# A batched fp32 matmul fed by one DMA queue: loads and stores queued in turns of four batches instead of one by one

## The chip, the cores and the metric

The kernel runs on one core of a Trainium2 chip, alone. The metric is device time in microseconds for one launch: 261.9 us before the change (median of three runs, 261.72 to 262.05). One execution was also recorded by the hardware profiler; it took 262.47 us, of which the profile shows a span of 260.7 us from the first to the last instruction.

## The reference

Sixteen independent products, each of a transposed 768 x 512 matrix with a 768 x 1024 matrix, in fp32:

```python
batch, m, k, n = 16, 512, 768, 1024
x: (batch, k, m)   y: (batch, k, n)
return np.einsum('bkm,bkn->bmn', x, y).astype(np.float32)
```

Per batch x is 1536 KB, y is 3072 KB and the output is 2048 KB. Over the whole run 75.5 MB are read and 33.55 MB are written.

## The kernel before, in words

The kernel goes through the 16 batches in order. No scheduler is at work: each engine has its own list of instructions, written out by hand, and the engines meet at semaphores.

- **SP** issues all the DMAs, on one queue (L102 to L113). For each batch b it issues the load of x into one of two fp32 buffers `xs` (L106), the load of y into one of two buffers `ys` (L109) and, from batch 4 on (`LAG`), the store of batch b-4 (L111, the function `store` at L93). Stores 11 to 14 follow the last load (11 in the loop, the others in L112), and the store of batch 15 is issued after the section (L181). [...]
- **VectorE** casts x and then y of each batch to bf16 (L124, L128) into one of two slots of `xb` and `yb`, and counts each cast in the semaphore `cast`. The load of x for batch b waits for the cast of x of batch b-2 (L105), and the same holds for y (L108), since they share a buffer. The cast of x for batch b waits until the matmuls of batch b-2 are done (L122), since they read the slot.
- **GpSimd** only turns the count `cast` into the semaphore `ready` for TensorE (L131 to L134).
- **TensorE** does 48 matmuls per batch, of 128 x 128 weights with 512 columns (L150), in two groups of 24, each filling one half of PSUM (`ps`). It waits for `ready` (L141, L148) and, per group, for `room` (L145), which says that this half has been copied out. Each finished group adds one to `groups`.
- **ScalarE** copies each half from PSUM into one of five output buffers `ob` (L166). For batch b from 5 on it first waits for the semaphore `so` of the store of batch b-5 (L163), which used the same buffer.
- `store(b)` waits until the matmuls of batch b+1 are done (L97), which implies that batch b was copied out; for batch 14 it waits for `outs` (L99). Before the last store SP waits for the stores 11, 12 and 13 (L174, L175).

`wide_dma` (L69) issues a load with long rows: a packet of x or y is 48 KB (four rows of x, two of y), one of a store 16 KB.

Of the kernel before, what the change touches and what calls it, by code (L numbers as in the profile page):

```python
# [1 line left out]

_os.environ.setdefault("NEURON_RT_ULTRASERVER_MODE", "4")

# [2 lines left out]

# [5 lines left out]


@with_exitstack
def kernel(
    ctx: ExitStack,
    tc: tile.TileContext,
    x: bass.AP,
    y: bass.AP,  # L20
    out: bass.AP,
):
    nc = tc.nc
    P = 128
    FP32 = mybir.dt.float32
    BF16 = mybir.dt.bfloat16

    B, K, M = x.shape
    _, _, N = y.shape
    KT = K // P  # L30
    MT = M // P
    NF = 512
    NT = N // NF

    x_v = x.rearrange("b (p ko) m -> b p ko m", ko=KT)
    y_v = y.rearrange("b (p ko) n -> b p ko n", ko=KT)
    o_v = out.rearrange("b (p mo) n -> b p mo n", mo=MT)

    LAG = 4
    NO = 5
    KH = KT // 2

    section = ExitStack()
    section.enter_context(tc.tile_critical())
    ec = ctx.enter_context
    xs = [ec(nc.sbuf_tensor(f"xs{i}", [P, KT, M], FP32)) for i in range(2)]
    ys = [ec(nc.sbuf_tensor(f"ys{i}", [P, KT, N], FP32)) for i in range(2)]
    xb = ec(nc.sbuf_tensor("xb", [P, 2, KT, M], BF16))  # L50
    yb = ec(nc.sbuf_tensor("yb", [P, 2, KT, N], BF16))
    ob = [ec(nc.sbuf_tensor(f"ob{i}", [P, MT, N], FP32)) for i in range(NO)]

    HB = MT // 2
    ps = [ec(nc.psum_tensor(f"ps{i}", [P, HB, NT, NF], FP32)) for i in range(2)]
    sx = [ec(nc.semaphore(f"sx{i}")) for i in range(2)]
    sy = [ec(nc.semaphore(f"sy{i}")) for i in range(2)]
    so = [ec(nc.semaphore(f"so{i}")) for i in range(NO)]
    cast = ec(nc.semaphore("cast"))
    ready = ec(nc.semaphore("ready"))  # L60
    room = ec(nc.semaphore("room"))
    groups = ec(nc.semaphore("groups"))
    idle = ec(nc.semaphore("idle"))
    outs = ec(nc.semaphore("outs"))


    made = {}

    def wide_dma(key, dst, src, dram_rows, load):  # L69


        if key not in made:
            made[key] = nc.sync.dma_start(dst, src)
            return made[key]
        pat = mybir.BassSymbolicTensorAccessPattern
        widen = lambda a: a.rearrange("(q r) k m -> q (r k m)", r=dram_rows)
        plain = lambda a: a.rearrange("p k m -> p (k m)")
        s, d = (widen(src), plain(dst)) if load else (plain(src), widen(dst))
        return nc.sync.add_instruction(_copy.replace(
            made[key].ins, name=nc.get_next_instruction_name(),  # L80
            ins=(pat(ap=s.ap, dtype=s.dtype, bass_ap=s, is_dma=False),),
            outs=(pat(ap=d.ap, dtype=d.dtype, bass_ap=d, is_dma=False),),
            sync_info=None, ant_dge_precooked=False))


    def parts(b):
        return 2 if b in (15,) else 1


    nx = [sum(1 + parts(a) for a in range(b)) + 1 for b in range(B)]  # L90


    def store(b):  # L93


        if b < B - 2:
            nc.sync.wait_ge(groups, 2 * (b + 2))  # L97
        else:
            nc.sync.wait_ge(outs, b - (B - 3))  # L99
        nc.sync.dma_start(o_v[b], ob[b % NO][:]).then_inc(so[b % NO], 16)  # L100

    for b in range(B):  # L102
        i = b % 2
        if b >= 2:
            nc.sync.wait_ge(cast, nx[b - 2])  # L105
        wide_dma("x", xs[i][:], x_v[b], 4, True).then_inc(sx[i], 16)  # L106
        if b >= 2:
            nc.sync.wait_ge(cast, nx[b - 2] + parts(b - 2))  # L108
        wide_dma("y", ys[i][:], y_v[b], 2, True).then_inc(sy[i], 16)  # L109
        if b >= LAG:  # L110
            store(b - LAG)  # L111
    for b in range(B - LAG, B - 1):  # L112
        store(b)  # L113


    for _ in range(60):
        nc.vector.sem_inc(idle, 1)
    for b in range(B):
        i = b % 2
        n = 16 * (b // 2 + 1)  # L120
        if b >= 2:
            nc.vector.wait_ge(groups, 2 * (b - 1))  # L122
        nc.vector.wait_ge(sx[i], n)
        nc.vector.tensor_copy(xb[:, i], xs[i][:]).then_inc(cast, 1)  # L124
        nc.vector.wait_ge(sy[i], n)
        for h in range(parts(b)):
            ks = slice(h * KT // parts(b), (h + 1) * KT // parts(b))
            nc.vector.tensor_copy(yb[:, i, ks], ys[i][:, ks]).then_inc(cast, 1)  # L128


    for b in range(B):  # L131
        nc.gpsimd.wait_ge(cast, nx[b]).then_inc(ready, 1)
        for h in range(parts(b)):
            nc.gpsimd.wait_ge(cast, nx[b] + h + 1).then_inc(ready, 2 // parts(b))  # L134


    x_w = xb[:].rearrange("p s k (j mo) -> p s k mo j", mo=MT)
    pe = OrderedEngineSet([nc.tensor.engine])
    with nc.Fori(0, B // 2, engines=pe):
        with nc.Fori(0, 2, engines=pe) as s:  # L140
            nc.tensor.wait_ge(ready, 2).then_inc(ready, -2)  # L141
            for mo in range(MT):
                g, m = divmod(mo, HB)
                if m == 0:
                    nc.tensor.wait_ge(room, 1).then_inc(room, -1)  # L145
                for kt in range(KT):
                    if mo == 0 and kt == KH:
                        nc.tensor.wait_ge(ready, 1).then_inc(ready, -1)  # L148
                    for nt in range(NT):
                        mm = nc.tensor.matmul(  # L150
                            ps[g][:, m, nt], x_w[:, bass.ds(s, 1), kt, mo],
                            yb[:, bass.ds(s, 1), kt, nt * NF:(nt + 1) * NF],
                            start=(kt == 0), stop=(kt == KT - 1))
                if m == HB - 1:
                    mm.then_inc(groups, 1)


    nc.scalar.nop().then_inc(room, 2)
    for _ in range(60):
        nc.scalar.sem_inc(idle, 1)  # L160
    for b in range(B):
        if b >= NO:
            nc.scalar.wait_ge(so[b % NO], 16 * (b // NO))  # L163
        for g in range(2):
            nc.scalar.wait_ge(groups, 2 * b + g + 1)
            cp = nc.scalar.copy(ob[b % NO][:, g * HB:(g + 1) * HB].rearrange("p m (t f) -> p m t f", f=NF),  # L166
                                ps[g][:])
            if b < B - 1:
                cp.then_inc(room, 1)
        if b == B - 2:  # L170
            nc.scalar.drain().then_inc(outs, 1)
    cp.then_inc(outs, 1)

    for b in range(B - LAG - 1, B - 2):  # L174
        nc.sync.wait_ge(so[b % NO], 16 * (b // NO + 1))  # L175
    section.close()

    nc.sync.dma_start(o_v[B - 1], ob[(B - 1) % NO][:])  # L181


# [1 line left out]
_INS = ['x', 'y']  # L185
_OUTS = [((16, 512, 1024), 'float32')]


# [23 lines left out]
```

## Time and profile before

| | |
|---|---|
| median of three runs | 261.9 us |
| the profiled execution | 262.47 us |
| its span | 260.7 us |
| DMA queue of SP | 109.05 MB, 98.1% of 16 engines' span |
| mean rate | 418 GB/s |
| TensorE matmul busy | 186.1 us (71%) |
| VectorE busy | 82.0 us (31%) |
| ScalarE busy | 61.1 us (23%) |
| mean granted TensorE clock | 0.911 |
| y load, x load, store: median issue to landing | 28.2, 29.7, 32.6 us |

The page divides the span into 40 slices and gives a digit of busy share for each engine and for the DMA engines. The timeline lists instructions by start time; the bracket behind a row gives how long the engine had been idle and what ended that. A cast that was released by "DMA ys<-in_y_dram" starts just as the y load has landed, so the start times of the casts are a clock for the queue.

### The profile page before, as it was taken

How to read it: one execution, taken by the hardware profiler on the slowest of the kernel's cores; microseconds unless marked ns; L12 is line 12 of the kernel's file. 1: busy time of each engine (PE TensorE's matmuls, PEld its weight loads, DVE VectorE, ACT ScalarE, POOL GpSimd, SP SyncE). 2: the span in 40 equal slices, each digit the busy share in tenths (PEclk: the TensorE clock that was granted, in tenths of full speed). 3: DMA queues.
4: the chain of work that ended last, by engine and by line, in shares of the span. 5: the costliest groups of instructions: out<-in, count | busy, mean ns of one | idle time of the engine just before them, and what ended most of it. 6: DMA issues, size and time to landing. Idle time of an engine off the chain costs nothing. (4 is left out here: it accounts for less than half of the span.)

```text
span 260.7 us, 2506 instructions
## 1 busy us (share of the span) xinstructions
PE 186.1 (71%) x768; PEld 89.8 (34%) x768; DVE 82.0 (31%) x33; ACT 61.1 (23%) x33; POOL 0.2 (0%) x4
## 2 busy tenths in 40 slices
PE   0009999998937949479596894969959197696910
PEld 0004555554512515124242351434425043253500
DVE  0261644525222252312524115252142522225000
ACT  1000442243220222202214022040322205022220
POOL 0000000000000000000000000000000000000000
PEclk9999999999995999959889797797999889799985
DMA  7998999999899899989999989999998999999994
GB/s 260 432 494 385 468 385 468 392 392 488 385 410 493 370 450 475 427 385 405 483 400 437 465 367 453 410 483 402 410 485 382 445 468 417 410 410 430 427 410 181
DMA packets 4514, 109.07 MB, mean 418 GB/s; under 512 B 768, under 2 KB 768, under 8 KB 768
## 3 DMA queue, kind: packets, MB, share of 16 engines
q1 hardware_dynamic: 4512, 109.05, 98.1%
q14 instruction: 2, 0.02, 0.0%
HBM read 75.50 MB, written 33.55 MB: 418 GB/s over the span
## 5 line engine op out<-in xcount | busy, mean ns | idle before, releaser
L150 PE MATMUL ps<-yb,xb 128*128 x768 | 186.1, 407 | 62.7 <-PEq L145 60.7
L150 PEld LDWEIGHTS ps<-yb,xb 128*128 x768 | 89.8, 117 | 158.5 <-issue 92.2
L166 ACT COPY ob<-ps 128x2048 f32<-128x2048 f32 x32 | 59.8, 1870 | 184.2 <-PE ps L150 184.2
L128 DVE CAST yb<-ys 128x6144 bf16<-128x6144 f32 (+1 forms) x17 | 53.8, 3171 | 87.7 <-DMA ys<-in_y_dram 87.7
L124 DVE CAST xb<-xs 128x3072 bf16<-128x3072 f32 x16 | 28.2, 1760 | 69.4 <-DMA xs<-in_x_dram 65.3
L166 ACT ACT_TABLE_LOAD x1 | 1.3, 1283 | 5.3 <-issue 5.3
L196 POOL MEMSET const-bfloat16-1.0<- 128x1 bf16 x1 | 0.1, 102 | 0.0
L196 POOL MEMSET const-uint8-127<- 128x1 uint8 x1 | 0.1, 102 | 0.0
L196 POOL MEMSET const-float32-1.0<- 128x1 f32 x1 | 0.1, 99 | 0.0
L196 POOL MEMSET const-float32-0.0<- 128x1 f32 x1 | 0.1, 98 | 0.2 <-issue 0.2
## 6 DMA issues: line engine op xcount, KB each, us to landing
ys<-in_y_dram SPq DMA_DIRECT2D x16, 3072.0 KB, 28.2
out_dram<-ob SPq DMA_DIRECT2D x16, 2048.0 KB, 32.6
xs<-in_x_dram SPq DMA_DIRECT2D x16, 1536.0 KB, 29.7
```

The lines of the kernel that those rows point to most:

```text
L124: nc.vector.tensor_copy(xb[:, i], xs[i][:]).then_inc(cast, 1)
L128: nc.vector.tensor_copy(yb[:, i, ks], ys[i][:, ks]).then_inc(cast, 1)
L150: mm = nc.tensor.matmul(ps[g][:, m, nt], x_w[:, bass.ds(s, 1), kt, mo], yb[:, bass.ds(s, 1), kt, nt * NF:(nt + 1) * NF], start=(kt == 0), ...
L166: cp = nc.scalar.copy(ob[b % NO][:, g * HB:(g + 1) * HB].rearrange("p m (t f) -> p m t f", f=NF), ps[g][:])
L196: nc = _bacc.Bacc("TRN2", target_bir_lowering=False, num_devices=1)
```

## The change

SP's order of DMAs is rewritten. The loads of batches 0 to 7 come first. Then four stores (0 to 3), the loads of 8 to 11, the stores of 4 to 7, the loads of 12 to 15, and the stores of 8 to 15 follow in turn, the last of them after the section as before. Each load and each store keeps the waits that it had; five output buffers and two load buffers remain. The waits ahead of the last store name the same three stores. No other engine's instructions change.

```diff
-    LAG = 4
+    FIRST = 8
+    TURN = 4
     NO = 5
...
-    for b in range(B):
+    def load(b):
         i = b % 2
         if b >= 2:
             nc.sync.wait_ge(cast, nx[b - 2])
...
         wide_dma("y", ys[i][:], y_v[b], 2, True).then_inc(sy[i], 16)
-        if b >= LAG:
-            store(b - LAG)
-    for b in range(B - LAG, B - 1):
+
+    for b in range(B):
+        load(b)
+        if b + 1 >= FIRST and (b + 1 - FIRST) % TURN == 0:
+            a = b + 1 - FIRST
+            for c in range(a, a + TURN):
+                store(c)
+    for b in range(B - FIRST + TURN, B - 1):
         store(b)
...
-    for b in range(B - LAG - 1, B - 2):
+    for b in range(B - NO, B - 2):
         nc.sync.wait_ge(so[b % NO], 16 * (b // NO + 1))
```

## The prediction

> **What bounds the kernel now.** I read the page first, its DMA rows above all, then the casts in the timeline as a clock for the queue, then the queue in stretches of 2 us, and last the tail of the timeline.
>
> ```profile
> span 260.7 us, 2506 instructions
> PE 186.1 (71%) x768; PEld 89.8 (34%) x768; DVE 82.0 (31%) x33; ACT 61.1 (23%) x33; POOL 0.2 (0%) x4
> ...
> DMA  7998999999899899989999989999998999999994
> ...
> q1 hardware_dynamic: 4512, 109.05, 98.1%
> ```
>
> The one queue fills 98.1% of 16 DMA engines' span; no compute engine passes 71%. The queue is the bound from the first load to the last store. So the order of its transfers can move the time in three ways only: the queue runs dry, the same bytes take longer or shorter, or the last store is issued late.
>
> The casts of y start when the load of y has landed (rows of batches 3 to 8, then of 12 and 13):
>
> ```profile
> 48.18 3.36 DVE L128 CAST yb<-ys 128x6144 bf16<-128x6144 f32 x1 [4.49 <-DMA ys<-in_y_dram]
> ...
> 59.71 3.36 DVE L128 CAST yb<-ys 128x6144 bf16<-128x6144 f32 x1 [5.67 <-DMA ys<-in_y_dram]
> ...
> 76.28 3.36 DVE L128 CAST yb<-ys 128x6144 bf16<-128x6144 f32 x1 [6.18 <-DMA ys<-in_y_dram]
> ...
> 92.76 3.36 DVE L128 CAST yb<-ys 128x6144 bf16<-128x6144 f32 x1 [6.10 <-DMA ys<-in_y_dram]
> ...
> 108.57 3.36 DVE L128 CAST yb<-ys 128x6144 bf16<-128x6144 f32 x1 [5.44 <-DMA ys<-in_y_dram]
> ...
> 124.86 3.36 DVE L128 CAST yb<-ys 128x6144 bf16<-128x6144 f32 x1 [5.93 <-DMA ys<-in_y_dram]
> ...
> 188.27 3.36 DVE L128 CAST yb<-ys 128x6144 bf16<-128x6144 f32 x1 [5.45 <-DMA ys<-in_y_dram]
> ...
> 204.06 3.36 DVE L128 CAST yb<-ys 128x6144 bf16<-128x6144 f32 x1 [5.45 <-DMA ys<-in_y_dram]
> ```
>
> While only loads run (y of batches 1, 2 and 3 at 26.19, 37.18, 48.18) a batch takes 11.00 us for 4.72 MB, 429 GB/s. With a store in it, the best periods are 15.81 (92.76 to 108.57) and 15.79 (188.27 to 204.06), so a store takes 4.8 us for 2.10 MB, about the same rate; the packet records of the five stores at the end give 4.85. An undisturbed mixed period is thus the plain sum: passing between loads and stores costs nothing as such. But some periods are longer: 11.53 instead of 11.00 to batch 4, then 16.57, 16.48, 15.81, 16.29, 15.83, 15.95 and no excess after that. Against 15.81 the excess is 0.53 + 0.76 + 0.67 + 0 + 0.48 + 0.02 + 0.14 = 2.6 us. Where in the period it lies, the 2 us stretches show (last two columns: DMA share and GB/s):
>
> ```profile
> 54.00:56.00 2.00, 2.00 (x11) 1.04 (x10) 0.04 (x1) 0.15 (x1) 0.00 (x0) 1.00 1.15 467
> 56.00:58.00 2.00, 2.00 (x11) 1.08 (x10) 0.00 (x0) 0.53 (x1) 0.00 (x0) 1.00 0.77 270
> ...
> 72.00:74.00 2.00, 2.00 (x10) 0.91 (x8) 0.00 (x0) 0.00 (x0) 0.00 (x0) 1.00 0.73 295
> 74.00:76.00 2.00, 0.15 (x1) 0.00 (x0) 0.00 (x0) 1.82 (x1) 0.00 (x0) 1.00 0.90 385
> ```
>
> These dips are 2 to 4 us before the y load has landed on all 16 engines. The packet records of the trace place them: the first packet of the first store starts at 57.75, and the 14 y packets in flight then took 2.0 to 2.5 us instead of 1.82. At 73.6 it is the same with the second store. So the excess belongs to the switch from reading to writing: engines that are still reading are slowed as others begin to write. The switch back shows none (x behind a store lands 3.66 us later, behind another load 3.69).
>
> The tail:
>
> ```profile
> 223.82 12.24 PE L150 MATMUL ps<-yb,xb 128*128 x48 [4.01 <-PEq L145]
> ...
> 236.09 1.87 ACT L166 COPY ob<-ps 128x2048 f32<-128x2048 f32 x1 [3.25 <-PE ps L150]
> 238.03 10.72 PE L150 MATMUL ps<-yb,xb 128*128 x48 [1.97 <-ACT ob L166]
> ...
> 248.79 1.87 ACT L166 COPY ob<-ps 128x2048 f32<-128x2048 f32 x1 [3.26 <-PE ps L150]
> 250.88 0.33 SPq L181 DMA_DIRECT2D out_dram<-ob  x1
> ```
>
> The last store is issued at 250.88, about when the fastest engines finish store 14 (251.8 by the packet records); the slowest finish at 255.1. The queue never waits for it.
>
> [...] one y load lands over 1.2 us early in the run and 3.5 us late in it. [...]
>
> **The change part by part.** The sum is made on the profiled execution, 262.47 us, and carried over to the median 261.9 as a difference.
>
> *Bytes and packets* stay: cost 0.
>
> *Switches to writing.* Before, each of stores 0 to 11 follows a y load: 12 switches, 2.6 us in all. After, there are three: after the loads of 7, 11 and 15. What one costs at the new places isn't shown. From below: 0, as in about half of today's, which saves 2.6. From above: the dearest, 0.76 each, costing 2.3 and saving 0.3; or, if the cost goes by stores written and not by switches, all 2.6 stay and nothing is saved. Nothing in the trace makes a switch dearer than today's sum, since runs of five loads and of five stores show none. I take the mean of the first four, (0.53 + 0.76 + 0.67 + 0) / 4 = 0.49, since the later ones came when the engines had drifted apart: 3 x 0.49 = 1.5, **saved 1.1 us**.
>
> *Eight loads first.* This can cost by letting the queue run dry. I followed the order with the trace's durations: x 3.7, y 7.3, store 4.85, casts 1.76 and 3.36, a batch of matmuls 10.36 when back to back (copies of PSUM at 41.92 and 52.28) and 12.5 after idling (mean of eight such, 11.86 to 13.51). The y loads land 11.0 apart, batch 7's near 92. SP issues x(b) when x(b-2) is cast, so about one batch of loads, 11 us, is always queued ahead. TensorE at 10.4 to 11 keeps the pace. Then a new wait: ScalarE's copy of batch 5 (L163 of before) needs store 0, which used to be long gone and now lands behind y7, near 97. It blocks `room`, and with it the matmuls of 6, from about 85 until 99; they end near 111. The cast of x8 waits for them; x8 lands only near 115, behind four stores, so about 4 us remain, and behind it x9 and y9 are queued, another 11. The same happens with the copy of batch 9 and store 4, then PE batch 10 done about 4 us before x12 lands. **Cost 0**, hidden by 4 us of stores and 11 of queued loads.
>
> *SP.* Four stores are issued in a row at 0.59 us each; their waits (matmuls of batches up to 4 done) are met by about 75. Queued behind them on SP is x8, not needed by the DMA engines before 112. Cost 0.
>
> *The tail.* Store 8 is now behind y15, and the copy of batch 13 needs its buffer. Let T be the landing of y15. Store 8 lands at T + 4.9; copy 1.9; matmuls of 14 after long idling 12.5; of 15 back to back 10.4; last copy 1.9; issue 0.2: T + 31.8. The first packet of a transfer follows its issue by 1.0 (0.95 to 1.98 at the start): T + 32.8. Its turn on the slowest engine, behind stores 8 to 14, is T + 7 x 4.85 = T + 34.0. **Hidden, with 1.1 us to spare**; before, nobody waited for T. Stores 13 and 14 wait for matmuls done at T + 19.3 and a copy at T + 21.3, with turns at T + 24.3 and T + 29.1: hidden. What is late next if it fails is the last store, one for one.
>
> Sum: 262.47 - 1.1 = 261.4 on the profiled execution, 261.9 - 1.1 = **260.8** for the median.
>
> **Rivals.**
> *The stall goes nearly whole.* For it: seven of twelve switches cost under 0.15. Against: the first switch after a long run of loads, the likest to the new ones, cost 0.53, and the next two more. Price at today's mean, 2.6 / 12 = 0.22: 0.65 remain, 1.95 saved: 259.9.
> *The switch is not what counts,* but bytes written while an engine lags: all 2.6 stay, 261.9. For it: the lag of the slowest engine grows and the stalls end once it is large, as if it had to be paid once. Against: the dips begin with the first packets of a store.
> *The tail decides, slower.* The copy of 13 waits for store 8, TensorE idles some 13 us and starts cold. If batch 14 takes the worst cold 13.5 (+1.0) and batch 15 also runs at the cold 12.5 (+2.1), the chain is 3.1 longer, 2.0 more than its 1.1 to spare: 260.8 + 2.0 = 262.8. It makes the kernel slower by over 0.2% only if the chain is more than 2.7 us longer than I have it. Against: batch 0 warmed up within its first group and batch 1 followed at 10.4.
> That the change doesn't do what it says is out: SP's list shows the new order.
>
> **How the numbers follow.** This kernel can be told from no change at about 0.2%, 0.52 us: faster is under 261.4, slower over 262.4. Forecast, 260.3 to 261.3: 0.45. Stall nearly gone, 259.4 to 260.3: 0.20. Nothing saved, 261.4 to 262.3: 0.22. Tail decides, over 262.4: 0.13. So faster 0.65, the same 0.22, slower 0.13. Most of the chance is of one sign, and the range reaches from the whole stall gone (261.9 - 2.6 = 259.3, taken as 259.4) to nothing saved plus 0.4 for the spread of the runs and a tail that is a little late, 262.3; about 0.13 lies outside.
>
> **What would show it.** In the changed kernel's casts, y1 to y7 should be 11.0 apart with no dip; dips only near the starts of stores 0, 4 and 8, at most 0.8 us each; x8 at once behind store 3, some 19.4 + 3.7 us after y7. ScalarE should show waits on DMA ahead of the copies of 5, 9 and 13. The DMA share should be 9 in all slices but the first and last. Wrong would be: a dip while only loads run, a slice of idle DMA near 110 or 175, a store row slower than 4.85 each, or the last store issued more than 33 us after y15 has landed.

## The result and the profile after

| | before | changed |
|---|---|---|
| median | 261.98 us | 260.68 us (260.58 to 260.72) |
| profiled execution | 262.47 us | 260.58 us |
| its span | 260.7 us | 258.8 us |

The ratio of the times is 0.9951, with a 95% interval of 0.9933 to 0.9968: faster by 1.3 us, 0.5%. The two profiled executions lie 1.89 us apart; the one of before was 0.5 us above the median of its kernel, the one of the changed kernel 0.1 below.

From the page of the changed kernel, the rows that carried the prediction:

```profile
span 258.8 us, 2506 instructions
...
DMA  7999989899999999999999989999899999999987
...
q1 hardware_dynamic: 4512, 109.05, 98.6%
```

The same packets and bytes fill 98.6% of a span that is 1.9 us shorter. The queue is still the bound, and no slice in the middle shows it dry.

From the timeline of the changed kernel, casts of y as the clock of the queue (batches 5 to 7, then 10 and 11, then 14 and 15; in both kernels each starts 0.02 to 0.03 us after the last of the 16 landing records of its load):

```profile
69.96 3.36 DVE L135 CAST yb<-ys 128x6144 bf16<-128x6144 f32 x1 [5.48 <-DMA ys<-in_y_dram]
...
80.94 3.36 DVE L135 CAST yb<-ys 128x6144 bf16<-128x6144 f32 x1 [5.47 <-DMA ys<-in_y_dram]
...
92.12 3.36 DVE L135 CAST yb<-ys 128x6144 bf16<-128x6144 f32 x1 [5.66 <-DMA ys<-in_y_dram]
...
144.57 3.36 DVE L135 CAST yb<-ys 128x6144 bf16<-128x6144 f32 x1 [2.80 <-DMA ys<-in_y_dram]
...
155.55 3.36 DVE L135 CAST yb<-ys 128x6144 bf16<-128x6144 f32 x1 [3.42 <-DMA ys<-in_y_dram]
...
207.87 3.36 DVE L135 CAST yb<-ys 128x6144 bf16<-128x6144 f32 x1 [4.07 <-DMA ys<-in_y_dram]
...
218.85 3.43 DVE L135 CAST yb<-ys 128x3072 bf16<-128x3072 f32 x2 [4.69 <-DMA ys<-in_y_dram]
```

In both kernels the landing records come in the order in which SP issued the 48 transfers: the first of the 16 of a transfer after the first of the one before it, and so on to the sixteenth. Batches are 10.98 apart while only loads run. The load ahead of the first store (92.12) came 11.18 after the one before it, 0.2 late; those ahead of the fifth and the ninth store came on time (10.98 each). So the three switches cost 0.2 us in all, where the twelve of before cost 2.6.

What that did shows at the very end. These are stretches of 1 us in the kernel before; the last two columns are the DMA share and GB/s, and one engine alone is a share of 1/16 = 0.06:

```profile
255.00:256.00 1.00, 0.00 (x0) 0.00 (x0) 0.00 (x0) 0.00 (x0) 0.00 (x0) 0.50 0.81 344
256.00:257.00 1.00, 0.00 (x0) 0.00 (x0) 0.00 (x0) 0.00 (x0) 0.00 (x0) 0.50 0.70 295
257.00:258.00 1.00, 0.00 (x0) 0.00 (x0) 0.00 (x0) 0.00 (x0) 0.00 (x0) 0.50 0.15 66
258.00:259.00 1.00, 0.00 (x0) 0.00 (x0) 0.00 (x0) 0.00 (x0) 0.00 (x0) 0.50 0.08 33
```

And the same stretches in the changed kernel:

```profile
255.00:256.00 1.00, 0.00 (x0) 0.00 (x0) 0.00 (x0) 0.00 (x0) 0.00 (x0) 0.50 1.04 442
256.00:257.00 1.00, 0.00 (x0) 0.00 (x0) 0.00 (x0) 0.00 (x0) 0.00 (x0) 0.50 1.23 524
257.00:258.00 1.00, 0.00 (x0) 0.00 (x0) 0.00 (x0) 0.00 (x0) 0.00 (x0) 0.50 0.01 0
258.00:259.00 1.00, 0.00 (x0) 0.00 (x0) 0.00 (x0) 0.00 (x0) 0.00 (x0) 0.50 0.00 0
```

Before, a share of 0.15 and then 0.08 is left: two engines or so, then one, work on after the others are done. In the landing records of the last store (when each engine reported its part as done) the middle one of 16 engines is through at 257.08 and the slowest at 259.90. In the changed kernel all are through between 257.82 and 258.02. Both spans end 0.79 us after the last landing, so each kernel ends with its slowest DMA engine, and in the changed kernel that engine no longer lags.

The new wait, from the list of waits of the changed kernel, and the tail, from its timeline:

```profile
ACT ob L173 <- DMA out_dram<-ob: 60.1, 3, 21.7
```

```profile
223.74 3.63 ACT L173 COPY ob<-ps 128x2048 f32<-128x2048 f32 x2 [19.83 <-DMA out_dram<-ob]
225.98 23.60 PE L157 MATMUL ps<-yb,xb 128*128 x96 [13.61 <-PEq L152]
...
249.61 1.87 ACT L173 COPY ob<-ps 128x2048 f32<-128x2048 f32 x1 [3.26 <-PE ps L157]
251.67 0.33 SPq L188 DMA_DIRECT2D out_dram<-ob  x1
```

ScalarE waits three times for a store, 60.1 us in all, ahead of the copies of 5, 9 and 13. Two of these stay hidden behind the queue. The third stands in the tail: the last store is issued at 251.67, 32.8 us after y15 has landed. Its first packet starts 0.05 us after the slowest engine's last packet of store 14, so the queue did run dry there for a moment, and the last store lands 5.03 us after store 14 instead of 4.85.

### The profile page after: what moved, and what is told of

Its sections match the earlier page's. It is cut to its first block, busy times and chain, and to the rows that moved or that the text cites. A ratio compares the mean times of both kernels' runs of the same rounds, so it can differ in the third digit from the quotient of the medians.

```text
span 258.8 us, 2506 instructions
## 1 busy us (share of the span) xinstructions
PE 181.6 (70%) x768; PEld 89.3 (34%) x768; DVE 82.0 (32%) x33; ACT 60.9 (24%) x33; POOL 0.2 (0%) x4
## 3 DMA queue, kind: packets, MB, share of 16 engines
q1 hardware_dynamic: 4512, 109.05, 98.6%
## 5 line engine op out<-in xcount | busy, mean ns | idle before, releaser
L157 PE MATMUL ps<-yb,xb 128*128 x768 | 181.6, 402 | 68.0 <-PEq L152 68.0
```

Of the source, the lines that this page charges most:

```text
L157: mm = nc.tensor.matmul(ps[g][:, m, nt], x_w[:, bass.ds(s, 1), kt, mo], yb[:, bass.ds(s, 1), kt, nt * NF:(nt + 1) * NF], start=(kt == 0), ...
```

## The experiments

The theory: engines that are still reading are slowed when others begin to write, and each switch from loads to stores adds to the lag of the slowest engine. Rivals: the eight loads ahead are what helps, not the number of switches; TensorE at work is what makes the stall (it was idle at all three switches of the changed kernel, from 84.4 to 99.2, 150.3 to 162.6 and 212.4 to 226.0 us); the price goes with something else than the count. A second question is whether the late last store costs anything.

### Fewer and more turns: e1 and e2

Edit against the changed kernel; e2 has `TURN = 2`:

```diff
-    TURN = 4
+    TURN = 1
```

> Eight loads first as in the changed kernel, but then store and load alternate one by one: nine switches from loads to stores instead of three, the same tail. If the number of switches sets the stall, at the mean of before, 0.22 us each, nine cost 2.0 us where the changed kernel shows 0.2: 1.8 us above it, 262.4 us, with dips in the DMA rate at the store starts. If it is the eight loads ahead that avoid the stall, and not the fewer switches: 260.7 us, as the changed kernel, and no dips.

> Eight loads first, then turns of two stores and two loads: five switches, the same tail. By number of switches, 5 x 0.22 = 1.1 us of stall, 0.9 above the changed kernel: 261.6 us. If the eight loads ahead are what counts: 260.7 us.

Measured: e1 261.61 us, ratio to before 0.9988 (0.9979 to 0.9996); e2 261.13 us, ratio 0.9968 (0.9955 to 0.9980). Both lie between what the two theories expected. The eight loads ahead alone explain neither; the time falls with the number of switches, 261.96 (12), 261.61 (9), 261.13 (5), 260.68 (3), at about 0.14 us for each. The intervals of e1 and e2 overlap a little, and so do those of e2 and the changed kernel (0.9933 to 0.9968); that of e1 lies apart from the changed kernel's. The tail of e1 shows a laggard again:

```profile
256.00:257.00 1.00, 0.00 (x0) 0.00 (x0) 0.00 (x0) 0.00 (x0) 0.00 (x0) 0.50 0.39 164
257.00:258.00 1.00, 0.00 (x0) 0.00 (x0) 0.00 (x0) 0.00 (x0) 0.00 (x0) 0.50 0.15 66
```

### Freeing the tail: e3 and e12

In e3 store 8 joins the second turn:

```diff
-            a = b + 1 - FIRST
-            for c in range(a, a + TURN):
+            first, last = {7: (0, 4), 11: (4, 9), 15: (9, 12)}[b]
+            for c in range(first, last):
                 store(c)
```

> The changed kernel, but store 8 joins the stores 4 to 7, ahead of the last four loads, so that the copy of batch 13 finds its buffer free; still three switches. If the last store of the changed kernel is late because TensorE waits for store 8, the copy of 13 loses its wait of 19.8 us, the last store is issued over 10 us earlier, and the end comes 0.2 us earlier, what the queue ran dry for: 260.4 us. If the gap ahead of the last store comes from something else: 260.7 us and the gap stays.

In e12 there is a sixth output buffer:

```diff
-    NO = 5
+    NO = 6
```

> The changed kernel with six output buffers: the copy of batch 13 no longer waits for store 8, and nothing else moves. If the 0.2 us for which the queue ran dry before the last store is a loss: 260.5 us. If the slowest DMA engine would have ended no earlier, as with store 8 moved ahead: 260.7 us.

Measured: e3 260.68 us, ratio 0.9953 (0.9941 to 0.9965); e12 260.78 us, ratio 0.9946 (0.9934 to 0.9958). Neither can be told from the changed kernel (0.9951). From the timeline of e3:

```profile
242.70 1.87 ACT L173 COPY ob<-ps 128x2048 f32<-128x2048 f32 x1 [3.25 <-PE ps L157]
248.88 0.33 SPq L188 DMA_DIRECT2D out_dram<-ob  x1
```

The last copy now ends at 244.6, 7 us earlier than in the changed kernel, and the last store is issued at 248.88, 0.65 us after store 13 has landed, for which SP waits. The expected 10 us earlier were too many, as that wait comes first: it is 2.8 us earlier. The queue no longer runs dry, and yet the last landing stays at 258.00. The middle engine is through at 256.81, 1.1 us earlier than in the changed kernel; the slowest isn't. So the late last store costs the changed kernel nothing that can be measured: it only makes 15 engines wait for what the slowest would have taken.

### Pushing the tail: e4

```diff
-    NO = 5
+    NO = 4
```

> The changed kernel with four output buffers instead of five. If the chain from store 8 over the copies and TensorE to the last store has no slack left, it now begins one batch earlier (the copy of 12 waits for store 8), holds three batches of matmuls instead of two, and the end is later by one batch, 10.4 us: 271 us. If the queue still hides it, as the prediction's 1.1 us of slack and the drift of the engines would let one think for small delays: at most 265 us.

Measured: 270.28 us, ratio 1.0321 (1.0296 to 1.0345). From its timeline, and its stretches of 2 us:

```profile
225.90 33.10 PE L157 MATMUL ps<-yb,xb 128*128 x144 [18.92 <-PEq L152]
...
261.10 0.33 SPq L188 DMA_DIRECT2D out_dram<-ob  x1
```

```profile
242.00:244.00 2.00, 2.00 (x11) 1.07 (x10) 1.42 (x1) 0.45 (x1) 0.00 (x0) 1.00 0.92 393
244.00:246.00 2.00, 2.00 (x11) 1.08 (x10) 0.00 (x0) 1.42 (x1) 0.00 (x0) 1.00 0.00 0
246.00:248.00 2.00, 2.00 (x11) 1.02 (x10) 0.00 (x0) 0.00 (x0) 0.00 (x0) 1.00 0.00 0
```

Three batches of matmuls now follow store 8, and the queue stands still while TensorE is busy. The chain that the prediction put in the tail is real, and the changed kernel stands right at the point from which it decides: one batch more costs 9.6 us.

### Doubling the switches, with halves of 64 partitions: e5 and e6

Stores 0 to 14 become two DMAs, back to back in e5; in e6 the first of them moves between the loads of x and y:

```diff
-    def store(b):
+    def store(b, h):
...
-        nc.sync.dma_start(o_v[b], ob[b % NO][:]).then_inc(so[b % NO], 16)
+        hs = slice(h * P // 2, (h + 1) * P // 2)
+        nc.sync.dma_start(o_v[b, hs], ob[b % NO][hs]).then_inc(so[b % NO], 16)
...
```

> The kernel before with stores 0 to 14 issued as two DMAs of 64 partitions each, back to back after the load of y: still twelve switches from loads to stores. It is the yardstick for the next kernel. If switches set the stall: as before, within 0.3 us of 261.96.

> As the yardstick, but the first half of each store is queued between the load of x and the load of y of the same batch, so that the queue passes from loads to stores 24 times. If each switch costs what the runs with 12, 9, 5 and 3 switches show, 0.14 us, this is 12 x 0.14 = 1.7 us above the yardstick, 263.6 us. If the stall belongs to something that happens once per batch, and not to the switch: as the yardstick, within 0.3.

Measured: e5 1.0465 times before (1.0425 to 1.0505), e6 1.0288 times (1.0249 to 1.0327). The yardstick itself was some 12 us slower, so the pair can't price a switch. Still, twice the switches made it faster and not slower, with intervals that lie apart; neither theory expected that. From e5's stretches of 2 us while its first store runs:

```profile
60.00:62.00 2.00, 2.00 (x11) 1.08 (x10) 2.00 (x1) 0.00 (x0) 0.00 (x0) 1.00 1.11 360
62.00:64.00 2.00, 1.45 (x8) 0.64 (x6) 0.51 (x1) 1.48 (x1) 0.00 (x0) 1.00 1.07 270
```

The engines are busy and move less: in the records 365 packets, loads and stores alike, took over 50 ns more than the median of their kind, against 64 in the kernel before.

### Doubling the switches, with halves of each row: e9 and e10

The same pair, but each half holds all 128 partitions and two of the four row blocks (8 KB packets). In e10:

```diff
...
-        nc.sync.dma_start(o_v[b], ob[b % NO][:]).then_inc(so[b % NO], 16)
+        hs = slice(h * HB, (h + 1) * HB)
+        nc.sync.dma_start(o_v[b][:, hs], ob[b % NO][:, hs]).then_inc(so[b % NO], 16)
...
         wide_dma("x", xs[i][:], x_v[b], 4, True).then_inc(sx[i], 16)
+        if b >= LAG:
+            store(b - LAG, 0)
...
-            store(b - LAG)
+            store(b - LAG, 1)
...
```

> The kernel before with stores 0 to 14 issued as two DMAs each, now halved along the row (8 KB packets, all 128 partitions in each), back to back after the load of y: twelve switches. The halves of 64 partitions were 12 us slower with the same twelve switches; if that came from which partitions an engine reads, this yardstick stays within 2 us of the kernel before (262 to 264 us); if it came from having two DMAs per store, it is some 10 us slower again.

> As that yardstick, with the first half of each store queued between the loads of x and y: 24 switches from loads to stores instead of twelve, the same packets. If each switch costs 0.14 us: 1.7 us above the yardstick. If the stall is paid once per batch, or only as the engines drift apart: within 0.5 us of it.

Measured: e9 (12 switches) 262.94 us, ratio 1.0029 (1.0018 to 1.0041); e10 (24 switches) 261.83 us, ratio 0.9990 (0.9977 to 1.0003). Twice the switches are 1.1 us faster, where 1.7 slower was expected. The theory of a price per switch falls. The e9 result says besides that two DMAs per store are not what made e5 slow (1.0029 against 1.0465); it was the halves of 64 partitions. The ends differ here too. From the 1 us stretches of e9, then of e10:

```profile
257.00:258.00 1.00, 0.00 (x0) 0.00 (x0) 0.00 (x0) 0.00 (x0) 0.00 (x0) 0.50 0.23 98
258.00:259.00 1.00, 0.00 (x0) 0.00 (x0) 0.00 (x0) 0.00 (x0) 0.00 (x0) 0.50 0.15 66
```

```profile
257.00:258.00 1.00, 0.00 (x0) 0.00 (x0) 0.00 (x0) 0.00 (x0) 0.00 (x0) 0.50 0.58 246
258.00:259.00 1.00, 0.00 (x0) 0.00 (x0) 0.00 (x0) 0.00 (x0) 0.00 (x0) 0.50 0.00 0
```

In e9 a few engines work on alone. In e10 most engines wait for the last store, which is issued late (251.82), and the slowest ends 1.2 us earlier than in e9. The packets that took over 50 ns too long add up to 1.10 us per engine in e9 and 0.84 in e10, which is not much less. The difference lies with the engines that lag, as is shown below.

### Without most of the matmuls: e7 and e8

```diff
-                for kt in range(KT):
+                for kt in (0, KH):
...
-                            start=(kt == 0), stop=(kt == KT - 1))
+                            start=(kt == 0), stop=(kt == KH))
```

e7 is the kernel before with this edit, e8 the changed kernel with it; each sum of 768 products is left incomplete.

> The kernel before with two of the six slices of k in each product (16 matmuls per batch instead of 48, the rest of the sum is left out); DMAs, casts and copies stay. If the stall is the DMA engines' own at a switch, it stays: the end within 0.5 us of 261.96, with dips at the starts of early stores. If it needs TensorE at work beside it (in the changed kernel TensorE was idle at all three switches): the dips go and the time falls to about 260.

> The changed kernel with the same four slices of k left out. The chain behind store 8 then has some 13 us of slack. By switches: about 1.3 us below the kernel before with few matmuls, 260.7 us; if the late last store had cost the changed kernel anything, up to 0.2 less. If TensorE is what makes the stall: no difference to the kernel before with few matmuls.

Measured: e7 262.14 us, ratio to before 1.0000 (0.9988 to 1.0012); e8 260.22 us, ratio 0.9925 (0.9910 to 0.9941). With a third of the matmuls the order of before is as slow as ever, and the changed order is faster by 1.9 us. So the gain doesn't need TensorE at work. e8 lies 0.5 us below the 260.7 that was expected, though its interval overlaps that of the changed kernel (0.9933 to 0.9968).

### Short packets: e11

```diff
-        if key not in made:
-            made[key] = nc.sync.dma_start(dst, src)
-            return made[key]
+        if load:
+            return nc.sync.dma_start(dst, src)
```

> The kernel before with plain loads (one partition per packet: 12 KB for x and 24 KB for y) instead of the long ones, twelve switches as before. If the stall belongs to the passing from reading to writing as such, it stays and the time is 262 us within 0.5. If it comes from the long load packets (an engine that still has a 48 KB packet in flight as others write), it shrinks and the time falls to about 260.5.

Measured: 262.40 us, ratio 1.0006 (0.9996 to 1.0015). The stall stays with packets of half the length and less, so the long packets are not its cause.

### What the runs say together

The landing records of the last store, beside the medians. The kernel before measured 261.96 beside e1 to e4, 262.15 beside e5 to e8 and 262.23 beside e9 to e12, so medians of different rows compare to a few tenths; the landings come from one profiled execution each.

```
kernel            switches  median us  middle engine  slowest engine
before                  12     261.98         257.08          259.90
e7 few matmuls          12     262.14         257.16          259.61
e9 row halves           12     262.94         257.50          260.07
e11 short packets       12     262.40         257.23          259.69
e1                       9     261.61         256.91          258.62
e2                       5     261.13         257.06          258.22
e10 row halves          24     261.83         258.06          258.84
changed                  3     260.68         257.92          258.02
e3 store 8 earlier       3     260.68         256.81          258.00
e12 six buffers          3     260.78         256.91          257.88
e8 few matmuls           3     260.22         256.98          257.48
```

Where the last store is not late, and outside e10, the middle engine is through within 0.5 us of 257 in every one of these orders. What the order moves is how far the slowest lags behind it: 2.5 to 2.8 us with twelve whole stores in between, 1.7 with nine, 1.2 with five, 0.5 to 1.2 with three. That is the gain on the profiled executions: from before to the changed kernel the last landing is 1.88 us earlier and the time 1.89 us shorter.

Where the lag comes from is seen in the packet records. In the kernel before, 64 load packets after the first batch took over 50 ns too long, and 54 of them were in flight as the first packet of a store started. The records don't name the engine. But of the 3439 packets that start after 19 us in the kernel before, 2740 start 3 or 4 ns before another one ends, and 659 of the others start 2 or 3 ns after such an end. Taking that other packet for the one ahead on the same engine, which is an inference, one can string the packets together in the order of the landings, with few doubtful links. This gives, for long packets after the first batch:

- In the kernel before, the engine that ends last is 0.7 us behind the middle one at the first load of y, ahead of any store. It then loses 3.1 us in six packets, all in loads of y with a store behind them (4, 5, 6 twice, 8 and 10). Two others lose 2.6 and 1.8, the remaining thirteen 1.3 at most.
- In e2 one engine has one long y packet at each of the four switches after the first, 1.2 us together, and no other engine has one there. This engine ends last.
- In e9 three engines lose 2.5 to 3.3 us each. In e10 again a few lose most, but none more than 1.9.
- In the changed kernel no engine loses more than 0.34 us. The y packets are long at the first switch only, though one engine is still 0.9 us behind at the others.
- The lag that is left in e3 and e12 grows in the stores and not at the switches. The engine that ends last there has at most one long packet (0.1 us), but its store packets take up to some 40 ns more than the 611 ns of the others, 1.1 and 1.3 us in all. In e8 no engine loses more than 0.4 us in this way.

So in the kernel before and in e2 the slowest engine loses its time (3.1 and 1.2 us) in reads that are under way as others begin to write, or just after, and the same few engines pay again and again. What slows these reads, why it is these engines, why the later switches of the changed kernel cost nothing, and why half stores after x and y cost the slowest less, stays open: no run here set the lag of an engine and left the rest as it was.

## Why the prediction was right

**The bound** was read rightly: one queue, filled from end to end before and after (98.1% and 98.6%). Loads alone ran at the same rate in both, a batch in 11.00 and in 10.98 us; that they could not run faster was not shown.

**Switches.** The direction and the place were right, the size was not. The term 3 x 0.49 = 1.5 for the switches that remain measured 0.2, so on the profiled executions 2.4 us were saved and not 1.1. The price was taken from the first four switches of before, but the three new ones come far apart, after long stretches of one kind, and e9 beside e10 shows that a price per switch is the wrong measure: 24 cost less than 12. The 2.6 us that I summed from the casts, which wait for the slowest engine, were mostly that engine's growing lag (3.1 us in its long packets) and not a loss of all (1.1 us per engine). I took the second store to be like the first; but there one packet was 0.8 us too long and the others 0.3 at most. And of the twelve switches eight, not seven, cost under 0.15. The rival that the stall goes nearly whole was nearest on this point, and the one that a lag is what is paid had a part of the cause.

The 2 us stretches that I showed as dips are weak evidence: in the changed kernel they show one too,

```profile
216.00:218.00 2.00, 0.00 (x0) 0.00 (x0) 0.00 (x0) 0.00 (x0) 0.00 (x0) 0.50 0.44 188
```

though no packet there is long and y15 lands on time. A packet of 48 KB took 1.83 us (median), nearly the length of a stretch of 2 us, so a stretch counts some too early or too late. The periods between casts and the packet records hold.

**Eight loads first** cost nothing, as predicted. ScalarE's copy of batch 5 began at 97.0 (97 predicted), the matmuls of 6 ended near 112.7 (111), x8 landed at 115.3 (115): 2.6 us to spare ahead of the queued loads, not 4.

**The tail** was mis-sized by 1.0: the chain from y15's landing to the last issue measured 32.8 for 31.8. The matmuls of 14 and 15 took 23.6 for 22.9, and TensorE began 0.4 after the copy, for which nothing had been set. It had been idle for 13.6 us, and the granted clock was 0.50 from 222 to 230 us, 0.63 in 230 to 232 and 1.00 in 232 to 234; in the kernel before, it was 0.50 from 78 to 84, where the matmuls of a batch began after 6.0 us of idling and took 12.6. The slack of 1.1 was used up, and the last store landed 0.2 late. e3 and e12 show that this costs no time, e4 that the next delay would cost in full. So the slower rival had a real chain, but it needed 2.7. One reading of the kernel before was wrong: the landings of store 14 begin at 251.56, not 251.8, while the first packet of the last store starts at 251.71. Eight engines had nothing to do there, for some 0.6 us at most, so the queue did wait for the last store. It cost nothing, as the slowest engine landed store 14 only at 255.1.

**The sum** came out close, 260.8 for 260.68, and that is in part luck, as terms offset each other. From the landings of the two profiled executions: start 0.1 earlier, y loads 2.2 faster (0.1 of it in the first), x loads 0.2 and stores 0.3 slower (0.2 of it the last one), together 1.9. Stores 13 and 14 landed 4.91 and 5.00 us after the ones before them, a sign of being wrong that the prediction named; in the changed kernel too one engine has the longer store packets (1.2 us in all), and it lands store 14 last. Of the 1.9 us the medians show 1.3, since the execution of before that was profiled was 0.5 slower than its median, and the prediction carried its 2.6 us over to the median undiminished.

## What to carry to other kernels

Where one queue is full from end to end, look at when each of the DMA engines ends, and not only at the mean share: both kernels here ended 0.79 us after the last landing of the slowest, and the orders of loads and stores that let one engine fall behind cost up to what it lagged, 2.8 us at most. Fewer, longer turns of stores helped here (261.61 us in turns of one, 261.13 of two, 260.68 of four) as long as there were buffers for them. A moved store also moves whatever waits for its buffer, so follow the last store back to the first one whose buffer it needs: here that chain used up all of its slack, and one buffer less cost 9.6 us.

## What had not been expected of the hardware

- A store in two halves of 64 partitions made the kernel 4.7% slower (1.0425 to 1.0505), while halves of all 128 partitions cost 0.3%. In the first case packets of loads and of stores alike took over 50 ns too long, 257 and 108 of them. Why the halves of 64 partitions are slower is not shown.
- More switches between reading and writing were faster in one pair: 24 (e10, 261.83 us) against 12 (e9, 262.94) gained 1.1 us.
- In e3 one DMA engine was slower than the rest at stores alone: 53 of its 128 store packets took over 620 ns, against 7 on the other fifteen engines together.
- Leaving out two thirds of the matmuls in the kernel before changed its time by nothing (1.0000).
